# Attention without GpSimd's sums, output transposes one row tile later, and another ring for loaded gate values

## The chip, the cores and the metric

One core of one Trainium2 chip runs the whole program. The metric is the device time of one execution in microseconds. Three runs of the kernel before gave 1447.67, 1447.7 and 1448.51, a median of 1447.7. The engines named below are TensorE (PE, with its weight loads PEld), VectorE (DVE), ScalarE (ACT), GpSimd (POOL), and the queue SP, which issues most DMAs.

## The reference, cut to what matters

One encoder layer over 1024 rows of width 1024, in float32. The parts around the change:

```python
proj = h @ w_in                              # h: normalised input, 1024 x 1024
z    = proj[..., OFF_Z:OFF_BETA]             # gate of the 4 GDN heads, 128 wide each
o_gdn = _rms_norm(_gated_delta_rule(...), gdn_norm_g) * silu(z)
fqkv = proj[..., OFF_FOX:OFF_F]              # 8 attention heads of 64
s = q_i @ k.T * scale + c_i[:, None] - c_all[None, :]     # forgetting term, causal mask
o_fox = _rms_norm(softmax(s) @ v, fox_norm_g)
mix = concatenate([o_gdn, o_fox]) @ w_out
h = _layer_norm(ALPHA * h + mix, ...)        # then MLP, gated embedding, layer norm
```

## The kernel before

Every float32 product is made from two parts: `hi` is the operand rounded to the PE's float32r, `lo` is what is left (`split_lo`, line 53: `lo = src - hi`). A product is three matmuls (hi·hi, hi·lo, lo·hi). So each operand costs one cast (`hi`) and one subtraction (`lo`).

The stages in order of time: input layer norm and embedding; projections with convolution and the gated delta rule (GDN) of four heads, up to about 397 us; forgetting attention ("fox") of eight heads, about 397 to 655 us; output projection `ps_mix` with layer norm, gate, MLP up and MLP down.

The instructions of each engine stand in one fixed order that a planner writes when the kernel is built: each traced instruction gets a priority (its place in the program unless a line shifts it), and the planner takes by priority what its own cost estimates hold to be ready, and hands out the buffers of rings in that order. On the chip each engine and each queue works strictly in that order. The projections that are not urgent have their priority put far back: `fox_proj` and `z_proj` (matmuls `fq`, `fk`, `gz`, line 218) fill the PE between urgent work, also during attention. The first five groups of `ps_mix` (line 950) do so at the end of attention.

Attention runs as a pipeline over steps (head h, row tile r), eight row tiles of 128 queries per head in the order 0, 1, 4, 5, 2, 3, 6, 7. At step i the loop at the end of the function emits

- `fox_a` of step i: scores into PSUM (lines 753, 754, 756), then DVE adds the forgetting term and takes the minimum (758), then ACT's exponential (761). When r is 2 it also calls `fox_start` of the next head;
- `fox_b` of step i-1: PE transposes of the weights into `ps_pt` (783), ACT cast to `pth` (785), DVE subtraction to `ptl` (line 54). The PSUM ring `pt` has two banks and is shared with `ps_ot` of `gdn_mix` and `ps_fx` of `fox_out`;
- `fox_c` of step i-2 when r is odd: the product with the values for two row tiles (797) into `ps_av`, ACT copy to `ot` (801), PE transposes of `ot` into `ps_oq` (804) and a DVE reduction into `osb` (805). `ps_av` and `ps_oq` share one PSUM bank (`av`, one buffer);
- after the last row tile of a pair of heads, `fox_pair` (root mean square norm of the pair; its last multiplication, line 48, is on POOL), and some steps later `fox_out` (transposes of `osb`, and hi and lo into `act_hi`, `act_lo`).

`fox_load` brings q and k of a head through the ring `qk_raw` (two buffers): `qa` is cast on ACT and its lower half subtracted on DVE (128 partitions hold hi and lo of 64 channels); `ka` is cast and `kl` subtracted on POOL. `fox_values` does the same for the values, with the subtraction on POOL.

`gdn_mix` finishes a GDN head at four places of the attention of heads 6 and 7: it loads the head's output `o` through the ring `qk_raw` and the gate values `szl` (written to DRAM by `z_proj`) through the ring `cv` (three buffers), transposes `o` into two `ps_ot` banks of ring `pt`, multiplies by the gate on DVE (`szl`, line 51), casts into `act_hi` and subtracts into `act_lo` on POOL. `act_hi` and `act_lo` are also the input of all projections, so these writes come after the last `gz` matmul. The ring `cv` is also that of `sz`, the gate values that `z_proj` computes and sends to DRAM; the ring `th` of the same pool (three buffers) holds the tanh values of the convolution.

`load_half` brings the output weights `wo` in eight pieces: DMA, ACT cast, POOL subtraction.

Of the kernel before, what the change touches and what calls it, by code (L numbers as in the profile page):

```python
# [8 lines left out]
F32 = mybir.dt.float32  # L9
# [4 lines left out]
ALU = mybir.AluOpType  # L14

P = 128
# [6 lines left out]
DH = 64  # L23
# [9 lines left out]
def _sl(i, n=P):  # L33
    return slice(i * n, (i + 1) * n)
# [3 lines left out]
def tile_block(ctx: ExitStack, tc: tile.TileContext, x, p, ln_in_g, ln_in_b, w_in, conv_w, a_log, dt_bias,  # L38
               gdn_norm_g, b_f, fox_norm_g, w_out, ln1_g, ln1_b, w_up, w_down, w_ple, w_ple_gate,
               b_ple_gate, ln2_g, ln2_b, out):  # L40
    nc = tc.nc
    PS = bass.MemoryType.PSUM
    x, p, out = x[0], p[0, 0], out[0]
# [3 lines left out]
    def tt(eng, o, a, b, op):  # L47
        eng.tensor_tensor(out=o, in0=a, in1=b, op=op)

    def stt(o, a, s, b, op0, op1):  # L50
        nc.vector.scalar_tensor_tensor(out=o, in0=a, scalar=s, in1=b, op0=op0, op1=op1)  # L51

    def split_lo(eng, lo, src, hi):
        eng.tensor_tensor(out=lo, in0=src, in1=hi.bitcast(F32), op=ALU.subtract)  # L54
# [40 lines left out]
    act_hi, act_lo = [], []  # L95
# [127 lines left out]
    with tc.tile_pool(name="start", bufs=2, reuse_waits="tile") as stp:  # L223
# [83 lines left out]
        for t in range(NT):  # L307
            if t + 3 < NT:
                load_x(t + 3)
            h = stp.tile([P, D], F32, tag="h", name=f"h{t}")  # L310
# [106 lines left out]
    cp = cst.enter_context(tc.tile_pool(name="conv", bufs=2, reuse_waits="tile"))  # L417
# [42 lines left out]
    for i in range(1, 3):  # L460
        nc.sync.dma_start(out=img[i].rearrange("(q r i) -> q r i", q=32, i=P),
                          in_=zero[0:32].unsqueeze(1).to_broadcast([32, GH * HST // (32 * P), P]))
# [243 lines left out]
    fr = frs.enter_context(tc.tile_pool(name="foxr", bufs=2, side="right", reuse_waits="tile"))  # L706
# [3 lines left out]
    def fox_load(h):  # L710
        pr, j = h // 2, h % 2
        raw = [fp.tile([P, T], F32, tag="qk_raw", name=f"qkr{h}_{w}", bufs=2) for w in range(2)]
        for w in range(2):
            for half in range(2):
                nc.sync.dma_start(out=raw[w][_sl(half, 64)], in_=qk_spill[w, pr, _sl(j, 64), :])
        qa = fh[j].tile([P, T], F32R, tag="qa", name=f"qa{h}")
        ka = fh[j].tile([P, T], F32R, tag="ka", name=f"ka{h}")
        kl = fh[j].tile([P, T], F32R, tag="kl", name=f"kl{h}")
        nc.scalar.copy(out=qa, in_=raw[0])
        split_lo(nc.vector, qa[64:128], raw[0][64:128], qa[64:128])  # L720
        nc.gpsimd.tensor_copy(out=ka, in_=raw[1])
        split_lo(nc.gpsimd, kl, raw[1], ka)
        cb = fh[j].tile([P, T], F32, tag="cb", name=f"cb{h}")
        nc.sync.dma_start(out=cb, in_=row_spill[32 + h * 8:40 + h * 8, :].rearrange("c i -> (c i)").partition_broadcast(P))
        return qa, ka, kl, cb

    def fox_values(pr):
        raw = fp.tile([P, 8, 2, DH], F32, tag="qk_raw", name=f"vr{pr}", bufs=2)
        nc.sync.dma_start(out=raw.rearrange("q t a d -> q t (a d)"),
                          in_=v_spill[:, _sl(pr)].rearrange("(t q) c -> q t c", q=P))  # L730
        va = []
        for j in range(2):
            va.append(fvp.tile([P, 8, 2, DH], F32R, tag="va", name=f"va{pr}_{j}", bufs=3))
            nc.scalar.copy(out=va[j][:, :, 0], in_=raw[:, :, j])
            split_lo(nc.gpsimd, va[j][:, :, 1], raw[:, :, j], va[j][:, :, 0])
        return va

    heads, pairs, tiles = {}, {}, {}
# [49 lines left out]
    def fox_c(h, g):  # L788

        j = h % 2  # L790
        nk = 2 * g + 2
        va, osb, _ = pairs[h // 2]
        pth, ptl = tiles.pop((h, "c", g))
        po = psf.tile([P, 512], F32, tag="av", name="ps_av", bufs=1)
        for kb in range(nk):
            for i, pt in enumerate((pth, ptl)):
                nc.tensor.matmul(po[:, 0:256], va[j][:, kb].rearrange("q a d -> q (a d)"),  # L797
                                 pt[:, kb].rearrange("q a b -> q (a b)"),
                                 start=(kb == 0 and i == 0), stop=(kb == nk - 1 and i == 1))
        ot = fr.tile([P, 256], F32, tag="ot", name="ot")  # L800
        nc.scalar.copy(out=ot, in_=po[:, 0:256])
        pq = psf.tile([P, 512], F32, tag="av", name="ps_oq", bufs=1)
        for i in range(2):
            nc.tensor.transpose(pq[:, _sl(i)], ot[:, _sl(i)], ident)
        nc.vector.tensor_reduce(out=osb[:, 2 * g:2 * g + 2, j], in_=pq[:, 0:256].rearrange("q (r a d) -> q r d a", a=2, d=DH),
                                op=ALU.add, axis=mybir.AxisListType.X)

    def fox_pair(pr):
        _, osb, ls = pairs[pr]
        lsf = ls.rearrange("q r a -> q (r a)")  # L810
        o16 = osb.rearrange("q r a d -> q (r a) d")
        ss = fr.tile([P, 16], F32, tag="ss", name="fss")
        fn = fr.tile([P, 16], F32, tag="fn", name="fn")
        for q in range(4):
            sq = fr.tile([P, 4, DH], F32, tag="ot", name="fsq")
            nc.scalar.activation(out=sq, in_=o16[:, _sl(q, 4)], func=AF.Square)
            nc.vector.tensor_reduce(out=ss[:, _sl(q, 4)], in_=sq, op=ALU.add, axis=mybir.AxisListType.X)
        nc.vector.reciprocal(out=lsf, in_=lsf)
        tt(nc.vector, ss, ss, lsf, ALU.mult)
        tt(nc.vector, ss, ss, lsf, ALU.mult)  # L820
        nc.vector.tensor_scalar(out=ss, in0=ss, scalar1=1.0 / DH, scalar2=NORM_EPS, op0=ALU.mult, op1=ALU.add)
        rsqrt(fn, ss)
        tt(nc.vector, fn, fn, lsf, ALU.mult)
        tt(nc.gpsimd, o16, o16, fn.unsqueeze(2).to_broadcast([P, 16, DH]), ALU.mult)

    def fox_out(pr, bank=None):
        osb = pairs[pr][1]
# [20 lines left out]
    def gdn_mix(h):  # L848

        o = fp.tile([P, 8, P], F32, tag="qk_raw", name=f"o{h}", bufs=2)  # L850
        nc.sync.dma_start(out=o.rearrange("q c i -> q (c i)"), in_=o_spill[h])
        for half in range(2):
            s = cp.tile([P, 512], F32, tag="cv", name="szl", bufs=3)
            nc.sync.dma_start(out=s, in_=z_spill[h, :, _sl(half, 512)])
            ps = psf.tile([P, 512], F32, tag="pt", name="ps_ot")
            for i in range(4):
                nc.tensor.transpose(ps[:, _sl(i)], o[:, half * 4 + i], ident)
            stt(s, ps, gdn_gh, s, ALU.mult, ALU.mult)
            hi = act_hi[half][:, :, h]
            s = s.rearrange("q (t i) -> q t i", i=P)  # L860
            nc.scalar.copy(out=hi, in_=s)
            split_lo(nc.gpsimd, act_lo[half][:, :, h], s, hi)

    gdn_gh = cpool.tile([P, 1], F32, name="gdn_gh")
    nc.vector.tensor_scalar(out=gdn_gh, in0=gdn_g, scalar1=0.5, scalar2=None, op0=ALU.mult)
# [1 line left out]
    steps = [(h, r) for h in range(FH) for r in (0, 1, 4, 5, 2, 3, 6, 7)]  # L867
    fox_start(0)
    n = len(steps)
    later = {}  # L870
    for i in range(n + 12):
        if i < n:
            h, r = steps[i]
            fox_a(h, r)
            if r == 2 and h + 1 < FH:
                fox_start(h + 1)
            if h >= 6 and r in (1, 5):
                gdn_mix((h - 6) * 2 + r // 4)
        if 1 <= i <= n:
            h, r = steps[i - 1]  # L880
            fox_b(h, r)
            if r % 2:
                tiles[h, "c", r // 2] = tiles.pop((h, "p"))
        if 2 <= i < n + 2:
            h, r = steps[i - 2]
            if r % 2:
                fox_c(h, r // 2)
                if r == 7 and h % 2:
                    fox_pair(h // 2)
                    later[max(i + 8, n - 14 + 4 * (h // 2))] = h // 2  # L890
        if later.get(i, 3) < 3:
            fox_out(later[i])
    frs.close()
# [41 lines left out]
    def load_half(w, n, tiles, name):  # L935
        out = []
        for k2 in range(NK // 2):
            raw = wpool.tile([P, NK, P], F32, tag="w_raw", name=name + "_raw").rearrange("q a b -> q (a b)")
            raw = raw.rearrange("q (k c) -> q k c", c=512)
            nc.sync.dma_start(out=raw, in_=w[_sl(k2, 256), _sl(n, 512)].rearrange("(k q) c -> q k c", q=P))  # L940
            hi, lo = tiles[n, k2, 0], tiles[n, k2, 1]
            nc.scalar.copy(out=hi, in_=raw)
            split_lo(nc.gpsimd, lo, raw, hi)
            out += [(hi[:, i], lo[:, i]) for i in range(2)]
        return out

# [16 lines left out]
    with tc.high_priority(offset=LOOK):  # L963
        wo = [load_half(w_out, n, wot, f"wo{n}") for n in range(2)]
# [18 lines left out]
    for t in range(NT):  # L983
        h1 = hpool.tile([P, D], F32, tag="h1", name=f"h1_{t}")
        nc.sync.dma_start(out=h1, in_=h_spill[_sl(t), :])
        j = t % 4
# [431 lines left out]
    for js in ((0, 1), (2,), (3,)):  # L1418
        w = P * len(js)
        m = 512 // w  # L1420
        for c0 in range(0, NP, m):
            r = x0[:, count["r"] % 4]
# [49 lines left out]
```

## Time and profile before

| | |
|---|---|
| median of three runs | 1447.7 us |
| the profiled execution | 1447.75 us, its span 1446.0 us |
| PE busy | 1387.1 us (96%), 7342 matmuls |
| PEld busy | 1167.7 us (81%) |
| DVE busy | 1091.0 us (75%), 2290 instructions |
| ACT busy | 553.1 us (38%), 1016 instructions |
| POOL busy | 102.6 us (7%), 128 instructions |

The span is what the profiler's instruction records cover; the execution's own time is 1.75 us longer. The busy time of PE contains modelled ends of pipelined matmuls, so that a PE shown as busy may still have lost some time; its idle time, on the other hand, is lost wherever PE is the engine that everything waits for. Nearly all of POOL's work lies in the attention stage.

### The profile page before, as it was taken

The numbers are of one execution on the slowest core, as the hardware profiler recorded it, in microseconds if no ns is written. First come the engines' busy times: TensorE is split into PE (matmuls) and PEld (weight loads), VectorE is DVE, ScalarE is ACT, GpSimd is POOL, SyncE is SP. The second block draws the span as 40 slices with busy tenths as digits, with TensorE's granted clock in tenths as the row PEclk, the third lists the DMA queues.
The fourth block names the chain that finished last, engine by engine and source line by source line (L and its number), as shares of the span: only waits on it lengthen the run. The fifth ranks groups of instructions, "written<-read, shape, count | busy, mean of one in ns | idle before, by whom it ended". The sixth has DMA issues, their size and how long they took to land.

```text
span 1446.0 us, 20592 instructions
## 1 busy us (share of the span) xinstructions
PE 1387.1 (96%) x7342; PEld 1167.7 (81%) x7342; DVE 1091.0 (75%) x2290; ACT 553.1 (38%) x1016; POOL 102.6 (7%) x128
## 2 busy tenths in 40 slices
PE   7999989999999999699999999999999999999997
PEld 5988868988887777578889988888888888888885
DVE  6758899689378886657899776667777689757877
ACT  5223423241247765651124333233333444455421
POOL 1000000000024332440000000000000000000000
PEclk9999999999999999899999999999999999999999
DMA  9856435444553433432476764444444985334342
GB/s 303 252 167 208 124 92 134 130 162 125 146 156 88 124 97 114 131 124 88 153 267 199 214 215 147 139 145 159 155 160 164 310 302 185 96 101 131 110 139 80
DMA packets 195869, 229.10 MB, mean 158 GB/s; under 512 B 23877, under 2 KB 128566, under 8 KB 195766
## 3 DMA queue, kind: packets, MB, share of 16 engines
q1 hardware_dynamic: 186374, 221.48, 48.8%
q10 hardware_dynamic: 9008, 5.24, 1.4%
q8 instruction: 58, 0.95, 0.3%
q0 software_dynamic: 384, 1.06, 0.2%
q14 instruction: 45, 0.37, 0.1%
HBM read 152.14 MB, written 75.60 MB: 157 GB/s over the span
## 4 chain that ended last, share of the span: by engine, by line
PE 78%; DVE 9%; DMA 7%; issue 3%; ACT 2%; POOL 1%; SPq 0%; DVEq 0%; ACTq 0%; POOLq 0%
PE ps_uP L1204 21%; PE ps_da L1324 9%; PE ps_db L1324 9%; PE g L218 6%; PE ps_gP L1071 5%; PE ps_db L1430 3%; PE fk L218 3%; PE ps_mix L950 3%; PE psv L320 3%; PE ps_av L797 2%; PE fq L218 2%; PE gz L218 2%; PE ps_pt L783 2%; DVE h L51 2%; DVE cv L51 1%
## 5 line engine op out<-in xcount | busy, mean ns | idle before, releaser
L1204 PE MATMUL ps_uP<-T,uS 128*128 128x512 f32 x576 | 133.8, 390 | 0.0
L1204 PEld LDWEIGHTS ps_uP<-T,uS 128*128 128x128 f32 x576 | 108.0, 188 | 23.5 <-ACT ua L1209 0.2
L1294 ACT CAST rh<-rr 128x512 fp32r<-128x512 f32 x112 | 69.8, 623 | 141.5 <-PE ps_db L1324 47.9
L54 DVE TENSOR_TENSOR rl<-rr,rh 128x512 fp32r<-128x512 f32 x112 | 77.1, 690 | 57.0 <-ACT rh L1294 28.9
L1204 PE MATMUL ps_uP<-B,uA 128*128 128x512 f32 x384 | 92.2, 395 | 0.0
L950 PE MATMUL ps_mix<-wo,act_hi 128*128 128x512 f32 x256 | 83.0, 399 | 3.5 <-POOL wo L54 1.7
L1204 PEld LDWEIGHTS ps_uP<-B,uA 128*128 128x128 f32 x384 | 72.0, 188 | 17.3
L218 PE MATMUL g<-act_hi,in_hi 128*128 128x512 f32 x192 | 76.4, 398 | 5.0 <-DVE edge L431 5.0
L218 PE MATMUL g<-act_hi,in_lo 128*128 128x512 f32 x192 | 75.9, 397 | 0.6 <-DVE in_lo L54 0.6
L218 PE MATMUL g<-act_lo,in_hi 128*128 128x512 f32 x192 | 75.8, 395 | 0.0
L1294 ACT CAST rl<-B 128x512 fp32r<-128x512 f32 x96 | 59.5, 621 | 22.5 <-PE ps_db L1324 12.4
L54 DVE TENSOR_TENSOR uA<-uraw,uA 128x512 fp32r<-128x512 f32 x48 | 33.2, 692 | 46.0 <-ACT uA L1199 46.0
L1199 ACT CAST uS<-wS 128x512 fp32r<-128x512 f32 x64 | 39.4, 621 | 73.2 <-issue 48.2
L54 DVE TENSOR_TENSOR ql<-B,rl 128x512 fp32r<-128x512 f32 x96 | 65.9, 687 | 0.5 <-ACT rl L1294 0.2
L950 PEld LDWEIGHTS ps_mix<-wo,act_hi 128*128 128x128 f32 x256 | 47.5, 188 | 14.1 <-POOL wo L54 2.4
L783 PE MATMUL ps_pt<-ident,s 128*128 128x128 f32 x288 | 45.3, 277 | 14.1 <-DVE szl L51 8.9
L54 DVE TENSOR_TENSOR ptl<-ps_pt,pth 128x512 fp32r<-128x512 f32 (+2 forms) x96 | 50.9, 552 | 8.0 <-ACT pth L785 7.4
L761 ACT ACTIVATE s<-s,m 128x128 f32<-128x128 f32 (+3 forms) x64 | 50.0, 781 | 14.9 <-DVE m L758 11.4
L51 DVE SCALAR_TENSOR_TENSOR cv<-g,hcw,cv 128x510 f32<-128x510 f32 (+2 forms) x72 | 53.4, 741 | 1.0 <-ACT cv L424 0.5
L1324 PE MATMUL ps_db<-rl,rh 128*128 128x512 f32 x192 | 51.3, 389 | 0.0
L1324 PE MATMUL ps_db<-ql,rh 128*128 128x512 f32 x192 | 51.3, 389 | 0.0
L1324 PE MATMUL ps_db<-rl 128*128 128x512 f32 x192 | 51.3, 389 | 0.0
(369 smaller groups left out, 3675.5 us busy)
## 6 DMA issues: line engine op xcount, KB each, us to landing
uraw<-in_w_up_dram SPq DMA_DIRECT2D x32, 512.0 KB, 4.2
B<-in_w_down_dram SPq DMA_DIRECT2D x32, 512.0 KB, 5.9
rr<-rS SPq DMA_DIRECT2D x64, 256.0 KB, 2.7
in_raw<-in_w_in_dram SPq DMA_DIRECT2D x24, 512.0 KB, 4.3
rr<-rA SPq DMA_DIRECT2D x48, 256.0 KB, 2.9
h_spill<-h SPq DMA_DIRECT2D x16, 512.0 KB, 4.0
qkr<-qk_spill SPq DMA_DIRECT2D x32, 256.0 KB, 4.4
rA<-ub SPq DMA_DIRECT2D x32, 256.0 KB, 2.2
```

The source lines that it names most:

```text
L51: nc.vector.scalar_tensor_tensor(out=o, in0=a, scalar=s, in1=b, op0=op0, op1=op1)
L54: eng.tensor_tensor(out=lo, in0=src, in1=hi.bitcast(F32), op=ALU.subtract)
L218: mm = nc.tensor.matmul(ps, w[:, k, :], a[n][:, :, k], start=(k == 0 and wi == 0), stop=(k == NK - 1 and wi == 2))
L320: nc.tensor.matmul(ps[:, 0:264], a[t // 4][:, t % 4, k], w[:, k, _sl(n, 264)], start=(k == 0 and wi == 0), stop=(k == NK - 1 and wi == 2))
L761: nc.scalar.activation(out=s[:, :W], in_=s[:, :W], func=AF.Exp, bias=m[:, i:i + 1], scale=-1.0, accum_out=pairs[h // 2][2][:, r, j:j + 1])
L783: nc.tensor.transpose(pt[:, i], s[:, _sl(k0 + i)], ident)
L950: nc.tensor.matmul(ps, a[t // 4][:, t % 4, k], w, start=(k == 0 and wi == 0), stop=(k == NK - 1 and wi == 2))
L1071: nc.tensor.matmul(ps[j // 2][:, j % 2], B[b][s][k][:, _sl(j)], a[w][:, k], start=(first and j % 2 == 0 and k == 0 and wi == 0), stop=(j % ...
L1204: nc.tensor.matmul(ps[p], w[:, k], B[t][b][k], start=(chain is None and k == 0 and wi == 0), stop=(k == 3 and wi == 2), skip_group_check=c ...
L1294: nc.scalar.copy(out=hi, in_=src)
L1324: nc.tensor.matmul(ps[j], rs[x][:, _sl(j)], qs[y], start=(not chain and c == 0 and wi == 0), stop=(c == NP - 1 and wi == 2), skip_group_ch ...
L1430: nc.tensor.matmul(b[j], rs[x][:, i, _sl(j - js[0])], Q[c0 + i][y], start=(c0 == 0 and i == 0 and wi == 0), stop=(c0 + i == NP - 1 and wi ...
```

## The change

Every subtraction, cast and multiplication that the attention stage and the load of `wo` had on POOL goes to DVE or ACT (only the zero fills at lines 776 and 777 stay on POOL). The second half of `fox_c` becomes `fox_d`, one step later; `fox_pair` and the place where `fox_out` is entered are adjusted so that `fox_out` stays at the same step. `gdn_mix` takes the ring `th` for `szl`.

```diff
@@ fox_load
-        nc.gpsimd.tensor_copy(out=ka, in_=raw[1])
-        split_lo(nc.gpsimd, kl, raw[1], ka)
+        nc.scalar.copy(out=ka, in_=raw[1])
+        split_lo(nc.vector, kl, raw[1], ka)
@@ fox_values
-            split_lo(nc.gpsimd, va[j][:, :, 1], raw[:, :, j], va[j][:, :, 0])
+            split_lo(nc.vector, va[j][:, :, 1], raw[:, :, j], va[j][:, :, 0])
@@ fox_c
-        ot = fr.tile([P, 256], F32, tag="ot", name="ot")
+        ot = tiles[h, "o", g] = fr.tile([P, 256], F32, tag="ot", name="ot")
         nc.scalar.copy(out=ot, in_=po[:, 0:256])
+
+    def fox_d(h, g):
+
+        j, osb, ot = h % 2, pairs[h // 2][1], tiles.pop((h, "o", g))
         pq = psf.tile([P, 512], F32, tag="av", name="ps_oq", bufs=1)
         for i in range(2):
             nc.tensor.transpose(pq[:, _sl(i)], ot[:, _sl(i)], ident)
@@ fox_pair
-        tt(nc.gpsimd, o16, o16, fn.unsqueeze(2).to_broadcast([P, 16, DH]), ALU.mult)
+        tt(nc.vector, o16, o16, fn.unsqueeze(2).to_broadcast([P, 16, DH]), ALU.mult)
@@ gdn_mix
-            s = cp.tile([P, 512], F32, tag="cv", name="szl", bufs=3)
+            s = cp.tile([P, 512], F32, tag="th", name="szl", bufs=3)
-            split_lo(nc.gpsimd, act_lo[half][:, :, h], s, hi)
+            split_lo(nc.vector, act_lo[half][:, :, h], s, hi)
@@ the loop over steps
                 fox_c(h, r // 2)
+        if 3 <= i < n + 3:
+            h, r = steps[i - 3]
+            if r % 2:
+                fox_d(h, r // 2)
                 if r == 7 and h % 2:
                     fox_pair(h // 2)
-                    later[max(i + 8, n - 14 + 4 * (h // 2))] = h // 2
+                    later[max(i + 7, n - 14 + 4 * (h // 2))] = h // 2
@@ load_half
-            split_lo(nc.gpsimd, lo, raw, hi)
+            split_lo(nc.vector, lo, raw, hi)
```

## Rows read from the trace of the kernel before

**Rows 1.** Busy time by stage: length, PE, PEld, DVE, ACT, POOL, PE clock, DMA.

```profile
420.00:560.00 140.00, 132.77 (x851) 108.62 (x849) 115.86 (x311) 94.90 (x224) 51.79 (x72) 1.00 0.38 112
560.00:660.00 100.00, 85.02 (x482) 68.77 (x481) 54.30 (x141) 48.95 (x101) 39.82 (x34) 0.95 0.37 116
...
800.00:1446.00 646.00, 636.81 (x2870) 526.11 (x2869) 479.48 (x833) 239.36 (x402) 0.00 (x0) 1.00 0.51 163
```

**Rows 2.** Waits of PE over the span: total us, times, longest.

```profile
PE ps_pt L783 <- DVE szl L51: 8.9, 1, 8.9
...
PE ps_pt L783 <- DVE ptl L54: 4.0, 4, 1.1
...
PE ps_mix L950 <- POOL wo L54: 1.7, 2, 1.4
...
PE ps_mix L950 <- ACT wo L942: 1.4, 1, 1.4
PE ps_oq L804 <- ACT ot L801: 1.1, 1, 1.1
```

**Rows 3.** Timeline of PE around the longest wait: start, duration, instruction.

```profile
577.57 0.39 PE L218 MATMUL gz<-act_hi,in_lo 128*128 128x512 f32 x1
586.88 0.45 PE L783 MATMUL ps_pt<-ident,s 128*128 128x128 f32 x1 [8.92 <-DVE szl L51]
...
588.89 1.91 PE L831 MATMUL ps_fx<-ident,osb 128*128 128x128 f32 x8
```

**Rows 4.** Short stretches around that wait, columns as in the first group.

```profile
580.00:585.00 5.00, 0.00 (x0) 0.00 (x0) 0.04 (x1) 0.00 (x0) 3.33 (x2) 0.58 0.57 175
...
588.00:590.00 2.00, 2.00 (x10) 1.74 (x9) 0.96 (x4) 1.42 (x5) 1.98 (x2) 0.50 0.22 62
590.00:592.00 2.00, 2.00 (x13) 1.86 (x12) 1.20 (x2) 1.36 (x2) 0.00 (x0) 0.73 0.69 186
```

**Rows 5.** Timeline of the queue SP: start, duration of the issue, transfer.

```profile
483.73 0.33 SPq L458 DMA_DIRECT2D z_spill<-sz  x1
...
540.01 7.62 SPq L851 DMA_DIRECT2D o<-o_spill  x2
...
581.05 0.32 SPq L851 DMA_DIRECT2D o<-o_spill  x1
581.47 0.86 SPq L854 DMA_DIRECT2D szl<-z_spill  x2
```

**Rows 6.** Groups of DVE and ACT that have the shapes of the moved ones.

```profile
L54 DVE TENSOR_TENSOR qa<-qkr,qa 64x1024 fp32r<-64x1024 f32 x8 | 17.1, 2131 | 0.3
...
L719 ACT CAST qa<-qkr 128x1024 fp32r<-128x1024 f32 x8 | 8.4, 1044 | 1.5 <-DMA qkr<-qk_spill 1.5
...
L54 DVE TENSOR_TENSOR in_lo<-in_raw,in_hi 128x1024 fp32r<-128x1024 f32 x4 | 4.9, 1223 | 2.3 <-ACT in_hi L190 2.3
...
L54 DVE TENSOR_TENSOR uA<-uraw,uA 128x512 fp32r<-128x512 f32 x48 | 33.2, 692 | 46.0 <-ACT uA L1199 46.0
```

**Rows 7.** POOL's groups in attention: busy us, mean ns, idle before, releasers.

```profile
L54 POOL TENSOR_TENSOR kl<-qkr,ka 128x1024 fp32r<-128x1024 f32 x8 | 20.0, 2505 | 0.6
L54 POOL TENSOR_TENSOR wo<-wo_raw,wo 128x1024 fp32r<-128x1024 f32 x8 | 18.9, 2377 | 12.5 <-PE ps_av L797 6.7 <-ACT wo L942 5.8
...
L54 POOL TENSOR_TENSOR va<-vr,va 128x512 fp32r<-128x512 f32 x8 | 10.3, 1294 | 17.4 <-ACT va L734 12.4 <-DVE ptl L54 4.8
L54 POOL TENSOR_TENSOR act_lo<-szl,act_hi 128x512 fp32r<-128x512 f32 x8 | 10.3, 1288 | 6.9 <-ACT act_hi L861 6.8
...
L721 POOL CAST ka<-qkr 128x1024 fp32r<-128x1024 f32 x8 | 8.3, 1042 | 176.4 <-PE ps_o L638 148.8 <-DMA qkr<-qk_spill 20.2 <-PE ps_sc L753 7.3
L48 POOL TENSOR_TENSOR osb<-osb,fn 128x1024 f32<-128x1024 f32 x4 | 7.6, 1904 | 8.2 <-DVE fn L48 8.2
```

**Rows 8.** Timeline of all engines at one small DVE instruction.

```profile
568.03 2.40 POOL L54 TENSOR_TENSOR wo<-wo_raw,wo 128x1024 fp32r<-128x1024 f32 x1 [3.23 <-ACT wo L942]
...
568.20 2.27 DVE L48 TENSOR_TENSOR nwt<-fn 128x16 f32<-128x16 f32 x1
```

More of the change, by code (lines that the diff above doesn't have):

```diff
@@ L791, in fox_c @@
         nk = 2 * g + 2
-        va, osb, _ = pairs[h // 2]
+        va = pairs[h // 2][0]
         pth, ptl = tiles.pop((h, "c", g))
```

## The prediction

> **What bounds the kernel now.** I read the stretches first. From 800 us on PE is busy 636.8 of 646 us and POOL does nothing, so nothing there can answer to the change. Attention is different: in 420 to 560 us PE shows 132.8 of 140 us busy and DVE already 115.9 of 140, or 83%; in 560 to 660 us PE has only 85.0 of 100 and DVE 54.3 [rows 1]. Then I read PE's own waits, because PE carries the chain and its idle time is what can be had back. One wait stands out: 8.9 us, a transpose that waits for the gated values `szl` on DVE. Behind it come 4.0 us of transposes that wait for the `ptl` subtraction, 1.7 and 1.4 us of `ps_mix` waiting for the output weights on POOL and ACT, and 1.1 us of the output transposes waiting for ACT's copy [rows 2]. The timeline of PE places the long one: the last `gz` matmul starts at 577.57, the next instruction at 586.88 [rows 3]. The clock tells a second price of it: granted 0.58 on average in 580 to 585 while PE did nothing, 0.50 (the level of 1.2 GHz) in 588 to 590, 0.73 in 590 to 592 [rows 4]. So the filler ran out and attention was stuck.
>
> Why it was stuck, from SP's queue: the first two loads of `szl` are issued at 581.47, directly behind a load of `o` issued at 581.05, although their `o` was fetched from 540.01 on and the second half of the first head's gate values had gone to DRAM at 483.73 [rows 5]. The ring `cv` was full of `sz` on their way out, and the two PSUM banks of ring `pt`, already filled with transposed `o`, could not be given back to `fox_b`.
>
> **The change part by part.** The sum is made against the profiled execution, 1447.75 us (span 1446.0 and 1.75 around it), which is the median 1447.7 within 0.1 us.
>
> *Ring `th` for `szl`.* No `th` tile is in use during attention, so the first three loads need no `sz` to leave. They can go out on SP behind the `o` of 540.01, and the gate product runs when PE has transposed. The two `pt` banks come back, and attention runs on beside the `gz` matmuls instead of after them. What is late next: the casts into `act_hi` wait for the last `gz` matmul in any case, a fourth `szl` waits for a `th` buffer, and `fox_out` may hold `pt` banks until those casts are done. I expect three or so such instructions of 0.6 to 0.7 us (`uA`'s 0.692 is the nearest DVE row [rows 6]) between the last `gz` and the next transpose: 2 us. The gap start to start is 9.31 less one matmul of about 0.23, so 9.1; gain 9.1 - 2.0 = 7.1, between 0 (the loads go no sooner) and 9.1. Of the low clock, the work from 586.88 to 590 ran at half speed (loss 1.56) and in 590 to 592 at 0.73 (loss 0.54): 2.1 us [rows 4], which I count as regained, since the granted clock stayed at 1.00 through 420 to 560, where single waits of PE are about 1 us [rows 1, 2]; bounds 0 and 2.1.
>
> *POOL's sums to DVE.* Removed from POOL: 20.0 + 18.9 + 10.3 + 10.3 + 8.3 + 7.6 = 75.4 us [rows 7]. Added to DVE: `kl` and `wo`, 16 of 128x1024 at 1.223 (`in_lo`, same shape) = 19.6; `va` and `act_lo`, 16 of 128x512 at 0.692 = 11.1; `osb`, 4 of 128x1024, for which no DVE row has a broadcast operand, so `in_lo`'s 1.223 as well = 4.9 (POOL's 1.904 is the other end: 7.6). Together 35.5 us. Added to ACT: 8 casts at 1.044 = 8.4 us [rows 6].
>
> DVE also gets time back. Its `qa` subtraction has 1024 columns like `in_lo`, and takes 2.131 on average against 1.223 [rows 6]; 8 x 0.908 = 7.3 us. A multiplication of 16 columns took 2.27 us, ending when a POOL subtraction that began 0.17 us earlier ended [rows 8]; that is 2.1 more. So while POOL reads two operands, DVE's instructions of two SBUF operands stand still, and with POOL's sums this goes: 9.4 us. The Trainium skill says this of the two engines (SBUF — State Buffer, section Who interferes with whom: a DVE instruction with two SBUF inputs contends with a GpSimd instruction that reads SBUF, and the later one blocks fully). By that rule the 9.4 us go whole; if the stretching came from SBUF traffic in general it would stay, and the DVE bill would be 35.5 instead of 26.1 net.
>
> Where it lands: in 420 to 560 DVE takes 6 `kl`, 8 `va` and 2 `osb` = 15.3 us, less five stretched `qa` (4.5 by the mean), so about +11 at most: 115.9 to 127 of 140, 91%. In 560 to 660 it takes the 8 `wo`, 8 `act_lo`, one `kl`, two `osb`: 19.0 less 3.0, so 54.3 becomes 70 of some 88. DVE is near its limit in the first stretch, with a margin, and not in the second. In PE's waits: the 4.0 us behind `ptl` are those in which a stretched `qa` stood ahead of it; now `qa`, `kl` and `va` stand there as three short pieces between which the planner can put `ptl`. I take 2.5 us back (bounds: 4.0 back; or 11 lost, all of DVE's added time in the first stretch on the path). The output weights: their subtraction falls from 2.377 to 1.223, the `w_raw` buffer is free sooner, and of 1.7 + 1.4 = 3.1 us I take 2.0 back (0 to 3.1). For queueing on the fuller DVE and ACT I charge 1.5 us (0 to 8.4, ACT's whole added time).
>
> *`fox_d` one step later.* PE's wait of 1.1 us for `ot` goes. Nothing is added; only the place moves. `ps_av` and `ps_oq` share one bank, so the next product now follows the reduction by one step instead of two. Some 64 steps fill about 240 us, so a step is about 3.7 us (estimate from the stretches [rows 1]), far more than two transposes and a reduction. Gain 1.0; were each of the 32 moved pieces to cost a wait like that 1.1, it would be 35 lost, and filler matmuls would have to be missing each time; I stay with the near end.
>
> Sum: 7.1 + 2.1 + 2.5 + 2.0 - 1.5 + 1.0 = 13.2 us. 1447.75 - 13.2 = 1434.5.
>
> **Rivals.**
>
> *The hole stays.* The planner may place the `szl` loads no earlier, or SP's order may still put them behind the late `o`, or the stuck banks may be those of `fox_out`. For it: SP issues in order, and `o` at 581.05 stood ahead of `szl` [rows 5]. Against: two of the `o` were already in. Then only 2.5 + 2.0 + 1.0 - 1.5 = 4 remain: 1443.7, range 1441 to 1446.
>
> *DVE becomes the bound.* With 91% in 420 to 560 the `ptl` subtraction and the minimum of the scores come late whatever their place. The 11 us added there then lie on the path, the 2.5 and 1.5 don't enter, and the hole's 9.2 and 3.0 of the rest are had: 1447.75 + 11 - 12.2 = 1446.6, between 1443 and 1450. For it: 83% before. Against: PE's waits name DVE for few microseconds there. The Trainium skill has a rule on this side (Perfetto Trace Analysis, section Optimizing Scalar/DVE Operations): when DVE is saturated, giving work to ScalarE or even GpSimd can make sense; the change does the opposite.
>
> *POOL's waits move to DVE, and it is slower.* POOL idled before the moved instructions without harm to anyone: 12.4 for `va`'s cast, 6.8 for `act_hi`'s, 6.7 + 5.8 for `wo` [rows 7], 31.7 us. On DVE the same wait holds up `ptl` and the score minimum queued behind it, and PE after them. If two thirds of it, 21 us, stand there with no filler, the time is 1447.75 - 13.2 + 21 = 1455.6; it is slower than before from 13 us on, at most 1466. For it: a DVE queue in fixed order and a planner that takes DMAs for faster than they are. Against: ACT, also in order, already waits for the same loads just ahead, and `ptl` needs ACT too.
>
> **Chances.** Forecast 0.56 (its own range 1427 to 1441), hole stays 0.18, DVE the bound 0.13, waits on DVE 0.13. About 0.2%, 2.9 us, is what a measurement here can tell from no change. Faster: all of the first, most of the second (0.14) and a third of the third (0.04): 0.74. Same: 0.04 + 0.08 + 0.01 = 0.13. Slower: 0.13. The range takes in the larger regain at one side (all bounds: 9.1 + 2.1 + 4.0 + 3.1 + 1.1 = 19.4, and some microseconds for another order of the filler) and the DVE case at the other: 1425 to 1450.
>
> **What would show it.** Right: the `szl` loads issued soon after the first `o`; no PE wait over 3 us in attention and a granted clock of 1.00 there; `qa` near 1.22 on DVE; `ps_mix` no longer waiting for `wo`. Wrong: PE still idle after the last `gz`; PE's waits for `ptl` and the scores growing beyond 10 us; DVE's queue waiting for ACT's casts of `wo`, `va` or `act_hi` by more than 13 us while PE idles.

## The result and the profile after

The changed kernel takes 1428.49 us (median of four runs, 1426.32 to 1429.82) against 1448.11 us for the kernel before on the same chip: a ratio of 0.9861, 95% interval [0.9844, 0.9878], or 20.1 us less (19.6 by the medians). The forecast was 1434.5 us, with a range of 1425 to 1450. Direction and range were right; the gain was half as large again as the 13.2 us forecast, it is about as large as all the prediction's upper bounds together (19.4 us), and it came in other shares.

The profiled execution took 1429.82 us, with a span of 1427.9. First the busy times over the whole span:

```profile
PE 1381.4 (97%) x7342; PEld 1167.2 (82%) x7342; DVE 1106.8 (78%) x2326; ACT 560.7 (39%) x1024; POOL 29.6 (2%) x84
```

The span is 18.1 us shorter (1446.0 to 1427.9). PE ran the same 7342 matmuls in 5.7 us less busy time (1387.1 to 1381.4), so 12.4 us of the 18.1 are idle time that PE lost no more, and the rest lies in instructions shown as busy, among them those at a low clock. POOL gave up 73.0 us, ACT took on 7.6, and DVE only 15.8: 35.5 us of new instructions, less what others no longer stood still.

The same stretches as in [rows 1] and the first of [rows 4], columns as there:

```profile
420.00:560.00 140.00, 138.22 (x885) 115.11 (x884) 120.17 (x332) 102.00 (x233) 15.96 (x46) 1.00 0.40 123
560.00:660.00 100.00, 93.56 (x536) 77.54 (x535) 82.51 (x200) 49.22 (x100) 5.62 (x14) 0.98 0.38 125
580.00:585.00 5.00, 4.48 (x26) 3.83 (x25) 3.60 (x10) 2.26 (x6) 0.53 (x2) 0.70 0.47 154
```

Read the second column, PE's busy time. It rose in both stretches: by 5.4 us in the first, where before PE was idle for 7.2 us in waits of 1.3 us and less, and by 8.5 us in the second, where the one wait of 8.9 us stood, called the hole below. DVE is busier in both and did not become the bound.

PE's waits in attention (395 to 660 us; total, times, longest), to set against [rows 2]:

```profile
PE ps_oq L808 <- ACT ot L801: 1.9, 2, 1.3
...
PE ps_sc L753 <- DVE m L758: 1.4, 1, 1.4
PE ps_pt L783 <- DVE ptl L54: 1.2, 1, 1.2
PE ps_pt L783 <- DVE fn L48: 1.1, 1, 1.1
```

The wait of 8.9 us for `szl` and those for `wo` are gone; the longest left is 1.4 us. SP's queue shows the loads of `szl` early, to set against [rows 5] (start, duration of the issue, transfer):

```profile
441.89 0.33 SPq L458 DMA_DIRECT2D z_spill<-sz  x1
443.95 0.33 SPq L858 DMA_DIRECT2D szl<-z_spill  x1
...
541.02 0.32 SPq L855 DMA_DIRECT2D o<-o_spill  x1
```

Three of them (443.95, 476.70, 490.28) go out 2.1 to 3.2 us behind a `z_spill`, and 51 to 97 us ahead of the first `o`; before, the first was at 581.47. The groups of DVE that answer to [rows 6, 7] (busy us, mean ns, idle before):

```profile
L54 DVE TENSOR_TENSOR qa<-qkr,qa 64x1024 fp32r<-64x1024 f32 x8 | 9.8, 1222 | 0.3
L54 DVE TENSOR_TENSOR kl<-qkr,ka 128x1024 fp32r<-128x1024 f32 x8 | 9.8, 1220 | 0.3 <-ACT ka L721 0.3
L54 DVE TENSOR_TENSOR wo<-wo_raw,wo 128x1024 fp32r<-128x1024 f32 x8 | 9.7, 1219 | 1.2 <-PE ps_av L797 1.2
L54 DVE TENSOR_TENSOR va<-vr,va 128x512 fp32r<-128x512 f32 x8 | 5.4, 686 | 1.8 <-ACT va L734 1.8
...
L48 DVE TENSOR_TENSOR nwt<-fn 128x16 f32<-128x16 f32 x12 | 2.1, 171 | 0.2
```

`qa` fell from 2131 ns to 1222, and `kl`, `wo` and `va` cost DVE about half of what they cost POOL.

Where the time went within the stage is seen by cutting the trace at the first score matmul of heads 6 and 7 (557 and 605 us before, 556 and 587 after) and counting the filler `gz` in each piece. Busy time of tile `gz` alone, columns as above without POOL; before:

```profile
420.00:557.00 137.00, 42.49 (x127) 22.17 (x127) 3.40 (x5) 3.04 (x5) 1.00 0.37 110
557.00:605.00 48.00, 15.85 (x65) 11.93 (x65) 2.05 (x3) 1.77 (x3) 0.89 0.44 132
```

and after:

```profile
420.00:556.00 136.00, 49.35 (x160) 28.31 (x160) 4.09 (x6) 3.57 (x6) 1.00 0.40 122
556.00:587.00 31.00, 9.90 (x32) 5.77 (x32) 1.20 (x2) 1.20 (x2) 0.94 0.47 145
```

Head 6 starts at nearly the same time, but 33 more matmuls of filler are done by then, and head 6 itself is 16 to 17 us shorter. At about 0.23 us per matmul the filler done earlier is some 7.5 us of this; the other 9 are the hole and its clock. So the gain has two sources, and only one of them is the hole.

### The profile page after: what moved, and what is told of

Read it like the earlier page. It is cut to its first block, busy times and chain, and to the rows that moved or that the text cites. A ratio compares the mean times of both kernels' runs of the same rounds, so it can differ in the third digit from the quotient of the medians.

```text
span 1427.9 us, 20552 instructions
## 1 busy us (share of the span) xinstructions
PE 1381.4 (97%) x7342; PEld 1167.2 (82%) x7342; DVE 1106.8 (78%) x2326; ACT 560.7 (39%) x1024; POOL 29.6 (2%) x84
## 4 chain that ended last, share of the span: by engine, by line
PE 47%; DMA 4%; DVE 4%; issue 1%; ACT 0%; SPq 0%; DVEq 0%; ACTq 0%
PE ps_uP L1212 21%; PE ps_da L1332 9%; PE ps_db L1332 9%; PE ps_db L1438 3%; PE ps_mix L958 2%; DMA hb<-h_spill 1%; PE ps_gP L1079 1%; DVE h L51 1%; DMA r<-t_spill 1%; PE ps_tr L965 1%; DMA h_spill<-h 1%; DMA h<-h_spill 1%; DVE gv L51 0%; DVE st L140 0%; DMA wo_raw<-in_w_out_dram 0%
## 5 line engine op out<-in xcount | busy, mean ns | idle before, releaser
L785 ACT CAST pth<-ps_pt 128x512 fp32r<-128x512 f32 (+2 forms) x96 | 43.5, 480 | 22.1 <-PE ps_pt L783 21.0
L1332 PE MATMUL ps_da<-ql,rh 128*128 128x512 f32 x192 | 51.3, 389 | 0.0
L1332 PE MATMUL ps_da<-rl 128*128 128x512 f32 x192 | 51.3, 389 | 0.0
```

Source lines behind the costliest of these rows:

```text
L785: nc.scalar.copy(out=hi, in_=pt[:, :kn])
L1332: nc.tensor.matmul(ps[j], rs[x][:, _sl(j)], qs[y], start=(not chain and c == 0 and wi == 0), stop=(c == NP - 1 and wi == 2), skip_group_ch ...
```

## The experiments

Each kernel ran beside the kernel before on one chip, and its ratio is against that. Gain is (1 - ratio) x 1448 us.

| kernel | median us | ratio [95%] | gain us |
|---|---|---|---|
| changed kernel | 1428.49 | 0.9861 [0.9844, 0.9878] | 20.1 |
| th_only | 1441.23 | 0.9950 [0.9936, 0.9963] | 7.2 |
| sums_only | 1433.55 | 0.9903 [0.9887, 0.9920] | 14.0 |
| foxd_only | 1447.33 | 1.0000 [0.9989, 1.0012] | 0.0 |
| after_cv | 1433.28 | 0.9900 [0.9885, 0.9914] | 14.5 |
| sums_th | 1429.95 | 0.9870 [0.9852, 0.9889] | 18.8 |
| after_reads | 1435.95 | 0.9911 [0.9893, 0.9929] | 12.9 |
| after_writes | 1427.52 | 0.9856 [0.9836, 0.9877] | 20.9 |
| kl_only | 1436.44 | 0.9917 [0.9897, 0.9937] | 12.0 |
| after_klpool | 1437.34 | 0.9924 [0.9911, 0.9938] | 11.0 |
| qa_pool | 1440.90 | 0.9945 [0.9931, 0.9958] | 8.0 |
| kl_th | 1433.84 | 0.9898 [0.9883, 0.9913] | 14.8 |
| after_wopool | 1429.87 | 0.9866 [0.9850, 0.9883] | 19.4 |

### Which part: the ring, the sums, fox_d

**th_only**, the kernel before with the ring alone:

```diff
-            s = cp.tile([P, 512], F32, tag="cv", name="szl", bufs=3)
+            s = cp.tile([P, 512], F32, tag="th", name="szl", bufs=3)
```

> The kernel before with one edit: szl takes the ring th. Theory A (the ring makes the hole): szl is loaded before head 6, PE's wait of 8.9 us for szl goes, the clock stays at 1.00, and the time falls by about 9, to 1439 (1436 to 1442); heads 0 to 5 keep their times. Theory B (the hole is the chain qa, kl on POOL, o on SP): the loads go early but another wait of 6 us or more stands in the same place, and the time is 1444 or more.

**sums_only**, the kernel before with the six edits from POOL to DVE and ACT (those of the change in `fox_load`, `fox_values`, `fox_pair`, `gdn_mix`'s `act_lo` and `load_half`), ring `cv` kept:

> The kernel before with POOL's sums and casts on DVE and ACT, ring and fox_c as before. Theory A: the hole stays at 6 us or more, qa falls to 1.22 us, heads 2 to 5 do some 30 more filler matmuls in the same time; as the filler then ends sooner in front of the hole, the time falls by only 3 to 8, to 1440 to 1445. Theory B: the hole goes with POOL's sums, and the time is 1432 or less. Theory C (fox_d gave what heads 2 to 5 gained): 1446 or more.

**foxd_only**, the kernel before with `fox_d` alone:

> The kernel before with fox_d alone. Theory A: within 2 us of the kernel before, since PE's wait for ot is 1.1 us in all and the hole stays. Theory C: heads 2 to 5 take some 30 more filler matmuls and the time falls by 4 or more.

**after_cv**, the changed kernel with `szl` back in the ring `cv`:

> The changed kernel with szl in the ring cv again. Theory A: a wait of PE for szl of 5 us or more is back in head 6, and about 9 us of the gain are lost: 1437 (1434 to 1441). Theory B: no such wait, 1430 or less.

**sums_th**, the changed kernel without `fox_d`:

> The changed kernel without fox_d: POOL's sums on DVE and ACT, and the ring th. Theory A: within 2 us of the changed kernel, as fox_d alone did nothing; it would be 1427 to 1431. If fox_d only helps where PE is otherwise free of waits: 1431 or more.

The ring alone brings 7.2 us, the sums alone 14.0, both 18.8, everything 20.1; `fox_d` brings nothing that can be measured. The stretches say where. First 420 to 560 us, then 560 to 660, of th_only:

```profile
420.00:560.00 140.00, 132.79 (x850) 108.61 (x850) 115.40 (x311) 94.96 (x224) 51.47 (x71) 1.00 0.38 117
560.00:660.00 100.00, 90.69 (x512) 73.73 (x512) 62.22 (x159) 48.58 (x101) 40.70 (x34) 0.98 0.33 111
```

and of sums_only:

```profile
420.00:560.00 140.00, 139.76 (x896) 115.95 (x895) 121.58 (x332) 102.26 (x235) 17.30 (x49) 1.00 0.38 117
560.00:660.00 100.00, 90.54 (x501) 73.65 (x500) 79.60 (x192) 49.16 (x99) 3.89 (x14) 0.95 0.35 116
```

The ring leaves the first stretch as it was (132.8 us of PE) and mends the second. The sums lift the first to 139.8, and mend a good part of the second as well. PE's longest wait in sums_only and in after_cv:

```profile
PE ps_pt L783 <- DVE szl L51: 4.9, 1, 4.9
```

```profile
PE ps_pt L783 <- DVE szl L51: 5.8, 2, 5.5
```

With the ring `cv` the hole is still there, but 5 us long where it was 8.9. In th_only no wait for `szl` is left; the longest single wait is now 2.3 us, `ps_mix` behind `act_lo` on POOL. Two of these runs missed what was expected of them: sums_only, at 1433.55 us, came between the ranges of theories A and B, and after_cv got its wait for `szl` back but lost 5.6 us instead of about 9. So the ring is what makes the hole (theory A), and the length of the hole depends on the sums as well (theory B): SP's queue in sums_only shows the loads of `szl` at 568.71 instead of 581.47, again directly behind a load into the ring `qk_raw`, whose buffers come free when the subtractions of q and k are done. (Before, that load was the `o` of 581.05, issued 0.02 us after a `kl` on POOL that ran from 578.69 to 581.03.) In sums_only:

```profile
568.16 0.44 SPq L715 DMA_DIRECT2D qkr<-qk_spill  x1
568.71 1.00 SPq L854 DMA_DIRECT2D szl<-z_spill  x2
```

### Why the sums bring so much

Theory A1: DVE's instructions with two SBUF operands stand still while POOL reads operands. Theory A2: POOL's results come later and the planner's order is another. Two kernels keep the changed kernel's order of instructions on PE, DVE, ACT and SP and add work on POOL whose result nobody reads.

**after_reads**, 16 useless subtractions of 128x1024 on POOL, two behind each `kl`:

```diff
-        split_lo(nc.vector, kl, raw[1], ka)
+        split_lo(nc.vector, kl, raw[1], ka); [tt(nc.gpsimd, scrap, ka.bitcast(F32), ka.bitcast(F32), ALU.subtract) for _ in range(2)]
```

> The changed kernel with two useless GpSimd subtractions of 128x1024 per head added (inputs ka, into a tile that nothing reads); nothing waits for them, and PE, DVE, ACT and SP have the same instructions in the same order. Theory A1 (what POOL's sums cost was DVE standing still while POOL reads two operands): kl, qa, va or the small DVE instructions beside them stretch by 1 us or more per head, PE's lost time in heads 2 to 5 comes back, and the time rises by 4 to 12 over the changed kernel, to 1432 to 1440. Theory A2 (it was the longer and later POOL results themselves, or the planner's order): within 2 us of the changed kernel's 1428.5.

**after_writes**, five useless memsets of the same tile instead (40 in all):

```diff
+        ...; [nc.gpsimd.memset(scrap, 0.0) for _ in range(5)]
```

> The control to the run with reads: five useless GpSimd memsets of 128x1024 per head, some 4.8 us of POOL as well, which read nothing. Theory A1: no DVE instruction stretches, and the time is within 2 us of the changed kernel's 1428.5. If any GpSimd work beside DVE costs, it is as slow as with reads.

POOL's added work in the two, then the DVE rows it met; after_reads:

```profile
L48 POOL TENSOR_TENSOR scrap<-ka 128x1024 f32<-128x1024 f32 x16 | 36.0, 2253 | 186.8 <-DMA in_raw<-in_w_in_dram 170.5 <-ACT ka L721 15.6
...
L54 DVE TENSOR_TENSOR kl<-qkr,ka 128x1024 fp32r<-128x1024 f32 x8 | 11.8, 1478 | 0.3 <-ACT ka L721 0.2
L48 DVE TENSOR_TENSOR nwt<-fn 128x16 f32<-128x16 f32 x12 | 3.5, 288 | 0.2
```

and after_writes:

```profile
L722 POOL MEMSET scrap<- 128x1024 f32 x40 | 38.2, 955 | 172.4 <-PE ps_o L651 170.9
...
L54 DVE TENSOR_TENSOR kl<-qkr,ka 128x1024 fp32r<-128x1024 f32 x8 | 9.9, 1232 | 0.3 <-ACT ka L721 0.2
L48 DVE TENSOR_TENSOR nwt<-fn 128x16 f32<-128x16 f32 x12 | 2.1, 171 | 0.2
```

As much POOL time in both; the reads cost 7.2 us against the changed kernel (20.1 - 12.9), the memsets nothing that can be measured (20.9). How a few stretched instructions become PE's loss is seen best on DVE's timeline at the same place of the two programs. The instructions of 16 columns are a chain of `fox_pair`; a `kl` and a `wo` of 1.22 us (left out) stand between them in both. The changed kernel:

```profile
575.72 0.17 DVE L48 TENSOR_TENSOR nwt<-fn 128x16 f32<-128x16 f32 x1
...
576.94 0.17 DVE L51 SCALAR_TENSOR_TENSOR nwt<-nwt,fss 128x16 f32<-128x16 f32 x1
...
578.25 0.68 DVE L54 TENSOR_TENSOR ptl<-ps_pt,pth 128x512 fp32r<-128x512 f32 x1
```

and after_reads, with POOL reading from 579.14 for 4.81 us:

```profile
579.14 4.81 POOL L48 TENSOR_TENSOR scrap<-ka 128x1024 f32<-128x1024 f32 x2 [9.82 <-ACT ka L721]
...
579.49 1.57 DVE L48 TENSOR_TENSOR nwt<-fn 128x16 f32<-128x16 f32 x1
...
582.12 1.86 DVE L51 SCALAR_TENSOR_TENSOR nwt<-nwt,fss 128x16 f32<-128x16 f32 x1
...
585.12 0.68 DVE L54 TENSOR_TENSOR ptl<-ps_pt,pth 128x512 fp32r<-128x512 f32 x1
```

Two instructions of 0.17 us became 1.57 and 1.86: 3.1 us. From the first of them to the `ptl` subtraction queued behind them it now takes 5.6 us instead of 2.5, 3.1 more, and PE's wait there grows from 1.1 to 4.2 us by the same 3.1:

```profile
585.95 0.87 PE L783 MATMUL ps_pt<-ident,s 128*128 128x128 f32 x3 [4.17 <-DVE fn L48]
```

That much of A1 is shown: with no other order of instructions and no later result that anything waits for, POOL's reads alone take microseconds from PE. In the kernel before the same group of rows stood at

```profile
L48 DVE TENSOR_TENSOR nwt<-fn 128x16 f32<-128x16 f32 x12 | 4.2, 347 | 0.2
L51 DVE SCALAR_TENSOR_TENSOR fn<-nwt,fn 128x16 f32<-128x16 f32 x12 | 3.8, 320 | 0.2
```

where the changed kernel has 171 and 167 ns: 3.9 us over both groups, besides `qa`'s 7.3 (8 x 0.909). With two smaller groups (2.2 us, of which 1.6 are one stretched one-operand `sso`) it is 13.4 us that DVE stood still; the prediction had counted 9.4 [rows 6, 8].

### Which of the sums

**kl_only**, the kernel before with the two `gpsimd` lines of `fox_load` alone moved to ACT and DVE:

> The kernel before with only ka on ACT and kl on DVE. Theory A1: qa falls to about 1.22 us, since kl was the POOL sum beside it, heads 2 to 5 do some 20 to 30 more filler matmuls, and more than half of what all sums gave comes: 1437 to 1441, with the hole for szl still there. Theory A3 (the output weights and act_lo give most): 1443 or more.

**after_klpool**, the reverse, the changed kernel with those two lines on POOL again:

> The changed kernel with ka and kl on POOL again. If kl is the sum that counts also with everything else in place: qa back to 2 us or more on average, heads 2 to 5 lose some 4 us more of PE's time, 1435 to 1440. If the six moved places are worth about the same each: 1430 to 1433.

**qa_pool**, the kernel before with more on POOL, `qa`'s subtraction too:

```diff
-        split_lo(nc.vector, qa[64:128], raw[0][64:128], qa[64:128])
+        split_lo(nc.gpsimd, qa[64:128], raw[0][64:128], qa[64:128])
```

> The kernel before with the subtraction of qa on POOL as well, so that kl can't hold it up on DVE; q and k of a head are then ready some 2 us later. If DVE standing still is what kl costs: PE's waits for ptl (4.0 us) fall under 2, and the time falls by 3 or more, to 1445 or less. If it is the late kl that costs: no gain or a loss, 1447 to 1452.

**kl_th**, kl_only with the ring `th`:

> The kernel before with kl and ka off POOL and the ring th, nothing else. If these two places make the change: 1428 to 1432, like the whole change. If va, act_lo, wo and osb matter by themselves: 1433 to 1437.

**after_wopool**, the changed kernel with the subtraction of `wo` on POOL again:

> The changed kernel with the subtraction of the output weights on POOL again, as a candidate: DVE was busy 19.4 of 20 us in 560 to 580 and would lose 9.8 us of work around there. If DVE bounds heads 6 and 7: 1424 to 1427, faster than the changed kernel. If PE's waits for the weights and the stretched DVE instructions come back: 1430 to 1433.

The stretch of 420 to 560 us, one row each for kl_only, after_klpool and qa_pool:

```profile
420.00:560.00 140.00, 138.90 (x896) 114.89 (x895) 114.91 (x322) 104.10 (x239) 33.37 (x59) 1.00 0.37 113
```

```profile
420.00:560.00 140.00, 131.72 (x844) 108.89 (x842) 119.88 (x319) 93.97 (x220) 37.29 (x61) 1.00 0.39 115
```

```profile
420.00:560.00 140.00, 135.21 (x868) 111.20 (x868) 107.82 (x309) 96.58 (x231) 60.04 (x79) 0.99 0.40 118
```

PE's busy time there goes with `kl`: 138.9 with it moved alone, 131.7 with it alone put back. `kl` and `ka` alone bring 12.0 us where all the sums bring 14.0, and putting them back costs 9.1 of 20.1. (kl_only came 0.6 us under the range of A1, and `qa`'s mean went to 1473 ns there and to 1670 in after_klpool, not to the 1.22 and 2 us expected: `osb` was still on POOL in the one, and in the other `fn` was hit in its place.) The other four sums add 2.0 (sums_only over kl_only) to 4.0 (sums_th over kl_th), at intervals that overlap; but the whole change lies 5.3 us below kl_th, at intervals that don't, so what is left beside `kl`, `ka` and the ring counts too, as the second range expected of kl_th has it. `wo` brings nothing that can be measured (19.4 against 20.1; the time lies between the two ranges that were expected), though PE waits 3.0 us for it there:

```profile
PE ps_mix L958 <- POOL wo L54: 3.0, 3, 1.4
```

qa_pool is the odd one: more work on POOL, and later `qa`, yet 8.0 us faster than before. It takes from DVE the instruction that stood still most, and PE no longer waits for `ptl` at all (4.0 us before). Since that also takes 17.1 us of work off DVE, it speaks for a DVE that holds PE up in the first stretch, and not for A1 alone. In qa_pool and in kl_only the hole is shorter as well (longest wait for `szl` 4.0 and 3.9 us), so their gains are not of the first stretch only.

How much of the first stretch is A1 can be read from the trace of the kernel before. PE's waits in 420 to 560 us are 4.0 us for `ptl` and 1.1 for `ot` [rows 2], and

```profile
PE ps_sc L753 <- DVE m L758: 1.3, 1, 1.3
PE ps_av L797 <- DVE osb L805: 0.6, 1, 0.6
```

Together they are 7.0 of the 7.2 us that PE is idle there, in seven waits. Ahead of six of them, 5.8 us in all, stands a DVE instruction that had stood still beside POOL's `kl` or `osb`, with DVE busy from there to the instruction that PE waited for: five times `qa` (at 445.97, 466.57, 492.73, 511.46 and 534.66), once a `fn` of 16 columns (at 488.73, 1.93 us instead of 0.17). The first of them:

```profile
445.25 2.40 POOL L54 TENSOR_TENSOR kl<-qkr,ka 128x1024 fp32r<-128x1024 f32 x1
445.97 2.77 DVE L54 TENSOR_TENSOR qa<-qkr,qa 64x1024 fp32r<-64x1024 f32 x1
449.52 0.66 PE L783 MATMUL ps_pt<-ident,s 128*128 128x128 f32 x4 [1.05 <-DVE ptl L54]
```

Each of the six lost 0.54 to 1.76 us that way, and none less than the wait behind it (to 0.01 us). The other kernels agree: in sums_only PE is idle for 0.2 us in this stretch; in kl_only two waits of 0.5 us are left, each behind a `qa` of 2.22 us beside POOL's `osb`; in after_klpool four waits of 1.3 to 1.5 us are back, each behind a `qa` or `fn` beside `kl` (a fifth, of 1.9, stands behind ACT). So A1 accounts for 5.8 of the 7.2 us. The useless reads take back only 2.2 us in this stretch (138.22 to 136.04); they met `kl` and small instructions there, but never `qa` (1222 ns in after_reads). The row of after_reads:

```profile
420.00:560.00 140.00, 136.04 (x859) 112.34 (x857) 124.25 (x322) 99.48 (x225) 47.09 (x63) 0.99 0.39 118
```

What is not settled is the other large part of the sums' gain, the hole that they shorten from 8.9 to 4.9 us. There a `kl` that is ready sooner (1.22 us on DVE for 2.5 on POOL) and the planner's other order can both be at work, and a kernel with the old order and `kl` ready sooner was not tried; this part of theory A2 stays open.

## Why the prediction was right, and where not

*The ring*: right in kind. The `szl` loads went out early, no PE wait is over 3 us, and th_only, with 7.2 us, lies below the 9.2 counted for hole and clock. On top of the sums it is 4.8 (sums_only to sums_th) and 5.6 us (after_cv to the changed kernel), since the sums had shortened the hole already; the prediction gave the hole to one cause, and it had two. One statement was wrong, there and in the description of `gdn_mix`: that "the casts into `act_hi` wait for the last `gz` matmul in any case". In the changed kernel the two halves of the rows are separate:

```profile
560.59 0.62 ACT L865 CAST act_hi<-szl 128x512 fp32r<-128x512 f32 x1 [1.52 <-DVE szl L51]
...
575.83 0.47 PE L218 MATMUL gz<-act_hi,in_lo 128*128 128x512 f32 x1
```

The cast stands 15 us before the last `gz`: the half it writes had been used up. So the 2.0 us charged behind the last `gz` were not due in that form.

*POOL's sums to DVE*: the step that was mis-sized. Taken as 2.5 + 2.0 - 1.5 = 3.0 us, they measured 14.0 alone and 11.6 on top of the ring (th_only to sums_th). The single costs were right: `kl` 1.22, `va` 0.69, `osb` 1.22 us, the stretched `qa` back at 1.22, DVE at 120 of 140 us where 127 was the upper guess. Wrong was what they were set against. The prediction booked the 9.4 us of DVE standing still as DVE's time, and as PE's time only 2.5 of the 4.0 us behind `ptl`. But the waits for `m` and `osb` had the same cause; in sums_only all of the stretch's 7.2 us of idle PE [rows 1] are gone but 0.2. The 33 `gz` matmuls done earlier, some 7.5 us, are about that time. Another 4.0 us are the part of the hole that the sums took away, which the prediction gave to the ring alone; together these are 11 of the 14.0 us; the rest was not taken apart. `wo`, given 2.0 of the 3.0, was worth 0.7, less than can be measured. That the 3.0 us that PE waits for it in after_wopool cost no more has two signs in its trace: PE's listed waits in attention add up to 10.4 us there against 7.9, only 2.5 more, and the granted clock stayed at 1.00 in 560 to 660, where the changed kernel's mean is 0.98.

That the total still came out nearer than its terms is in part luck: the ring brought 7.2 us alone and about 5 beside the sums, less than the 9.2 that it was given, and the sums more than four times what they were given. A gain as large as all upper bounds together (19.4 us) was not what the terms said; the range took it in because it was drawn some microseconds beyond them.

*fox_d*: 1.0 us forecast, none found. PE's wait for `ot` did not go, it is 1.9 us in the changed kernel.

*The clock*: the mean granted clock rose from 0.95 to 0.98 in 560 to 660, but in 580 to 585 it still is 0.70, with PE busy for 4.48 of 5 us there, behind waits of 1.1 and 0.9 us in 575 to 580. So up to 1.5 us (an estimate, 0.30 of 5 us) of the low clock's price remained; "1.00 in attention" was wrong, and the 2.1 us were not regained whole.

*The rivals*: the hole did not stay. DVE did not become the bound at 86% of the first stretch, and POOL's waits did not move: DVE idled 1.2 us before `wo` where POOL had idled 12.5, and 1.8 before `va` where POOL had 17.4 [rows 7].

The Trainium skill's rule of the two engines (SBUF — State Buffer, section Who interferes with whom: two-operand DVE instructions contend with GpSimd instructions that read, not with those that only write) agrees with both runs built for it, 7.2 us for the reads and none for the writes. The Trainium skill's other rule weighed there (Perfetto Trace Analysis, section Optimizing Scalar/DVE Operations) says that giving a saturated DVE's work to ScalarE or even GpSimd may make sense, and goes on that the two engines share an SBUF read port, so that moving work between them might not help. The warning is what this case shows: `ka` and `kl` on POOL cost 9.1 us with DVE at 86% (120.2 of 140) in the stretch.

## What to carry to other kernels

Work on an engine that seems free is not free where it makes another engine stand still, as POOL's reads did with DVE here (7.2 us for results that nobody read): compare the mean of DVE's small instructions with their shortest, and price every stretched one that stands ahead of what PE waits for. Before bounding a gain by one listed wait, ask of every wait in the stage what the engine waited for had done just before: here waits for `ptl`, `m` and `osb` had one cause, and the stage's whole idle time of PE was the bound. Two edits that act on one stall are each to be tried alone and together, since what one leaves sets the worth of the other.

## What the runs showed of the hardware beside this

POOL's memsets left DVE's two-operand instructions alone, but not its one-operand TENSOR_SCALAR. In after_writes, DVE and POOL at one place:

```profile
419.58 1.05 DVE L662 TENSOR_SCALAR sso<-sso 128x16 f32<-128x16 f32 x1
420.66 1.09 DVE L65 TENSOR_SCALAR ro<-sso 128x16 int32<-128x16 int32 x1
```

```profile
419.64 0.95 POOL L722 MEMSET scrap<- 128x1024 f32 x1
...
420.77 0.96 POOL L722 MEMSET scrap<- 128x1024 f32 x1
```

Instructions that take 0.17 us in the changed kernel lasted until the memset beside them ended, 1.05 and 1.09 us (and a third, of line 67, 1.09), while the TENSOR_TENSOR behind them, at 422.92, kept its 0.18. The Trainium skill has it that TENSOR_SCALAR can enter a mode that uses the port pair that DVE shares with GpSimd (SBUF — State Buffer, section Who interferes with whom); the rows agree. Here these 2.7 us cost nothing that can be measured (20.9 us of gain in after_writes, 20.1 in the changed kernel).
